# A third seven-product quad in the even gate/up blocks, and the down projection of a pair cut in two

## The chip, the core and the metric

One core of a Trainium2 chip runs the whole program. The metric is the device time of one execution in microseconds (us); several executions are timed and their median is given. Five engines matter. TensorE (PE) multiplies. VectorE (DVE) adds, subtracts and reads results out of PSUM. ScalarE (ACT) copies and applies functions. GpSimd (POOL) issues a few transfers. SyncE (SP) issues the weight loads. Each engine works through its own queue in a fixed order, and waits where an operand isn't ready.

## The reference, cut to what matters

Two decoder layers run over 256 tokens of width 2048 in float32. Each has a token mixer (sparse attention beside latent attention, not touched here), a layer norm, and a SwiGLU feed-forward part of width 5632 with a second layer norm:

```
def _swiglu(x, w_gate, w_up, w_down):
    h = jax.nn.silu(jnp.einsum('bsd,df->bsf', x, w_gate)) * jnp.einsum('bsd,df->bsf', x, w_up)
    return jnp.einsum('bsf,fd->bsd', h, w_down)
...
x = _layer_norm(ALPHA * x + mix, ln1_g[i], ln1_b[i])
ffn = _swiglu(x, w_gate[i], w_up[i], w_down[i])
x = _layer_norm(ALPHA * x + ffn, ln2_g[i], ln2_b[i])
```

## The kernel before

**Weights and units.** A float32 product is made of three matmuls of rounded parts: each operand is split in a high part and a rest, and high by high, high by rest and rest by high are summed. Weights come in units of 512 KB, two 128-row tiles of 512 columns. `load_raw` (L301) loads a unit from SP's queue into one of six `raw` buffers. `parts` (L308 and L309) makes `wh` on ACT and `wl` on DVE, into one of seven pairs of buffers (`UNITS` 5 and `MORE` 2). A unit against both token tiles is 12 matmuls of 512 columns, against one operand it is 6.

**Gate and up.** The 5632 hidden columns are done in eleven blocks `fc` of 512. Block 0 is done by `proj`. From block 1 on, `gate_up` takes the 2048 rows of weights in four quads. A quad is a 2 by 2 by 2 product: two token tiles, two row units `u` and `u + 4`, and the two columns gate and up. `plain_quad` does it with its eight products, as four weight units of 12 matmuls. `wino_quad` does it with seven products of 6 matmuls, `p1`, `p2`, `p5`, `p6`, `p7`, `p4`, `p3` in this order. For these, DVE forms four sums of raw weight units in place (`add`, L871), each weight operand is then split (seven pairs `wh`, `wl` where the plain quad has four), and the token operands `s1` to `s4` are sums made once for the layer by `sum_operands`. The order in a block is plain 0, wino 2, plain 1, wino 3.

**Ends of a block.** The products gather in eight PSUM banks, `c11` to `c22` and `p1` to `p7`. In the last quad of a block, eight DVE operations (L886 to L911, "finals" below) combine them: `g0` (L886) frees the bank `c11`, `g1` (L905) frees `c21`, and so on. The plain quad of the next block writes `c11` and `c21` first. `hidden` then applies silu (ACT), multiplies (DVE), transposes (PE) and splits the result to `hT`.

**Down.** After plain 0, `between` is called. In blocks 2, 4, 6 and 8 it runs `down` of the two finished blocks over all four output columns: 16 weight units of 12 matmuls. In the odd blocks nothing runs there. After block 10, `down` of blocks 8 and 9 runs over all columns, and `last_pass` does block 10.

**Sums.** `norm_T` leaves the transposed normalised `x` of chunks 1 and 3 in `kept`, two buffers of the `raw` tag, and until `sum_operands` has run, raw loads leave these two alone (`phase["held"]`). `sum_operands` runs between the gate and the up half of block 0.

The core of the quad loop is:

```
for i, (u, w) in enumerate(zip(plain, wino)):
    plain_quad(u, i == len(plain) - 1)
    if i == 0:
        between()
    r = wino_quad(w, i == len(wino) - 1)
```

Of the kernel before, what the change touches and what calls it, by code (L numbers as in the profile page):

```python
# [31 lines left out]
P = 128  # L32
D = 2048
# [24 lines left out]
RAWMORE = 2  # L58
HALF = NKT // KU // 2
T2 = 11  # L60
LASTU = 2


QI0, TA, QI1, TB, KA0, QA0, VA0, KA1, QA1, VA1 = range(10)
# [14 lines left out]
def hybrid_trunk(ctx: ExitStack, tc: tile.TileContext, x, xt_in, pos, w_in, g_cq, g_ckv, w_uq,  # L79
# [8 lines left out]
    def nm(s):  # L88
        uid[0] += 1
        return f"{s}{uid[0]}"  # L90
# [23 lines left out]
    def t2(shape, s, dt=F32):  # L114
        return sb.tile(shape, dt, name=nm(s), tag="t2", bufs=T2)
# [157 lines left out]
    def spawn(gen):  # L273
        task = [0, gen]
        tasks.append(task)
        step(task)
        return task
# [5 lines left out]
    def finish(*ends):  # L283
        while any(e in tasks for e in ends):
            for task in list(tasks):
                if any(e in tasks for e in ends):
                    step(task)


    def some(key, have, more):  # L290

        if phase["name"] == "more" and not (key == "raw" and phase.get("held")):
            phase[key] = phase.get(key, 0) + 1
            if phase[key] * more % (have + more) < more:
                return phase["pool"], more
        return sb, have
# [19 lines left out]
    def proj(units, lhs, n, before=None, split_t=None):  # L316

        o = [acc() for _ in range(NT)]  # L320
        loaded = []
        last = len(units) - 1

        def go(t, u):
            (wh, wl), ks = loaded[u], units[u][1]
            for j, k in enumerate(ks):
                h, l = lhs(t, k)
                a, b = wh[:, j, :n], wl[:, j, :n]
                first, final = u == 0 and j == 0, u == last and j == len(ks) - 1
                mm(o[t][:, :n], h, a, start=first, stop=False)  # L330
                mm(o[t][:, :n], h, b, start=False, stop=False)  # L331
                mm(o[t][:, :n], l, a, start=False, stop=final)  # L332

        for u, (src, ks) in enumerate(units):
            if before is not None:
                before(u)
            loaded.append(load_unit(src, src.shape[-1]))
            for t in range(1 if split_t else NT):
                go(t, u)
            tick()  # L340
        if split_t:
            split_t()
            for u in range(len(units)):
                go(1, u)
                tick()
        return o
# [5 lines left out]
    def split(hi, lo, src):  # L352
        nc.scalar.activation(hi, src, AF.Copy)
        nc.vector.tensor_tensor(lo, src, f(hi), op=ALU.subtract)  # L354
# [22 lines left out]
            nc.vector.tensor_scalar(y[:, sl], y[:, sl], mu, rs, ALU.subtract, ALU.mult)  # L377
            yield c, sl

    def norm_T(gbT, y, hi, lo, keep=None):  # L380


        for _ in normalise(y, moments(y)):
            pass
        yield 5
        for c in range(D // C):
            tp = trp()
            transpose4([y[:, c * C + i * P:c * C + (i + 1) * P] for i in range(4)], tp)
            if keep is not None and c in keep:
                v = keep[c]  # L390
            else:
                v = t2([P, 4, P], "v")
            for i in range(4):
                k = 4 * c + i
                nc.scalar.activation(v[:, i, :], tp[:, i * P:(i + 1) * P], AF.Identity,
                                     bias=gbT[:, 1, k:k + 1], scale=gbT[:, 0, k:k + 1])
            nc.vector.tensor_copy(hi[:, 4 * c:4 * c + 4, :], v)
            nc.vector.tensor_tensor(lo[:, 4 * c:4 * c + 4, :], v, f(hi[:, 4 * c:4 * c + 4, :]), op=ALU.subtract)
            yield 1
# [79 lines left out]
    def layer(l, xh, xl, norms, last):  # L479
# [296 lines left out]
        def then(t):  # L776
            xh.append(t8([P, NKT, P], F32R, "xh"))
            xl.append(t8([P, NKT, P], F32R, "xl"))
            norms.append(spawn(norm_T(gbT, xt[t], xh[t], xl[t], kept[t] if ffn[0] else None)))

        ffn, kept = [True], []
        phase["held"] = True
        for t in range(NT):
            v = phase["pool"].tile([P, 2, 4, P], F32, name=nm("kept"), tag="raw", bufs=RAWMORE)
            kept.append({1: v[:, 0], 3: v[:, 1]})
        last_pass(lambda c, k: w_o[l, c, k // KU], [4, 6], olhs, then)


# [2 lines left out]
        def gu(i, fc, split_t=None):  # L791
            return proj([(w_gu[i][l, fc, u], range(u * KU, (u + 1) * KU)) for u in range(NKT // KU)], xk, C,
                        None, split_t)
# [2 lines left out]

        def sum_operands():

            a = [[kept[t][c] for c in (1, 3)] for t in range(NT)]
            for name, x, y in (("s1", a[1][0], a[1][1]), ("s2", a[0][0], "s1"), ("s3", a[1][0], a[0][0]),  # L800
                               ("s4", a[0][1], "s2")):
                y = sums[y][2] if isinstance(y, str) else y
                v = t2([P, 4, P], "sv")
                nc.vector.tensor_tensor(v, x, y, op=ALU.subtract)
                hi, lo = (phase["pool"].tile([P, 4, P], F32R, name=nm(name), tag=name + p, bufs=1) for p in "hl")
                split(hi, lo, v)
                sums[name] = hi, lo, v
            phase["held"] = False

        def slhs(name):  # L810
            return lambda k: tuple(m[:, k % 4, :] for m in sums[name][:2])

        def hidden(gs, us, hT, tr):

# [16 lines left out]
        BANKS = {"c11": 4, "c21": 5, "c12": 6, "c22": 7, "p1": 0, "p5": 1, "p6": 2, "p7": 3}  # L831
        INTO = {"p2": "c11", "p4": "c21", "p3": "c12"}

        def gate_up(fc, plain, wino, between):


            o, begun = {}, set()
# [19 lines left out]
            def plain_quad(u, lastz):  # L857
                for i, col in enumerate(("c11 c21", "c12 c22")):
                    for v in (u, u + HALF):
                        w = load_unit(w_gu[i][l, fc, v], KU * C)  # L860
                        for t, name in enumerate(col.split()):
                            passes(name, token(t), unit(v), w, lastz and name == "c22" and v != u)
                        tick()
# [49 lines left out]
                if final:  # L913
                    return [g0, g1], [e, v]

            for i, (u, w) in enumerate(zip(plain, wino)):
                plain_quad(u, i == len(plain) - 1)
                if i == 0:
                    between()
                r = wino_quad(w, i == len(wino) - 1)  # L920
            return r

        def down(fcs, hTs, then):
            def lhs(t, k):
                h, j = hTs[k // 4], k % 4
                return h[:, 0, j, t * P:(t + 1) * P], h[:, 1, j, t * P:(t + 1) * P]

            units = C // P // KU * len(fcs)
            u0 = C // P // KU * fcs[0]
            if fcs[-1] == NFC - 1:  # L930
                units -= LASTU
            for c in range(D // C):
                o = proj([(w_down[l, c, u0 + u], range(u * KU, (u + 1) * KU)) for u in range(units)], lhs, C)
                for t in range(NT):
                    sl = xt[t][:, c * C:(c + 1) * C]
                    if fcs[0] == 0:
                        nc.vector.scalar_tensor_tensor(sl, sl, ALPHA, o[t], op0=ALU.mult, op1=ALU.add)
                    else:
                        d = t2([P, C], "d")
                        nc.scalar.activation(d, o[t], AF.Copy)  # L940
                        nc.gpsimd.dma_start(sl, d, accum_op=ALU.add)  # L941
            if fcs[-1] == NFC - 1:
                finish(*[h[2] for h in held])
                last_pass(lambda c, k: w_down[l, c, u0 + k // KU], [(units + i) * KU for i in range(LASTU)], lhs, then)

        def behind_ffn(t):
            if last:
# [10 lines left out]
        def free_banks(t):  # L958
            return bank(2 + t, "tr")

        def group():
            finish(*[h[2] for h in held])
            if len(held) == 2 and held[-1][0] < NFC - 2:
                down([h[0] for h in held], [h[1] for h in held], behind_ffn)
                held.clear()

        g = gu(0, 0, lambda: finish(*norms))
        sum_operands()
        affine(ln1_g[l], ln1_b[l], 0)
        u = gu(1, 0)  # L970
        affine(ln1_g[l], ln1_b[l], 1)
        spawn_hidden(0, g, u, free_banks)
        for fc in range(1, NFC):
            g, u = gate_up(fc, (0, 1), (2, 3), group)
            if fc == 1:
                affine(ln1_g[l], ln1_b[l], 2)
                affine(ln1_g[l], ln1_b[l], 3)
            spawn_hidden(fc, g, u, free_banks if fc < NFC - 1 else lambda t: trp())
        xh, xl, norms, ms = [], [], [], []
        ffn[0] = False  # L980
        if last:
            gb = [load_gb(ln2_g[l], ln2_b[l], slice(c * C, (c + 1) * C)) for c in range(D // C)]
        else:
            gbT = load_gbT(ln2_T[l])
        finish(*[h[2] for h in held[:2]])
        down([h[0] for h in held], [h[1] for h in held], behind_ffn)
        if last:
            for t in range(NT):
                norm_out(t, gb, ms[t])
# [57 lines left out]
```

## Time and profile before

| what | value |
|---|---|
| time, median of 3 runs | 2238.47 us (2237.68 to 2239.29) |
| profiled execution | 2240.56 us |
| its span, first to last instruction | 2238.5 us |
| PE busy | 2194.0 us, 98% |
| DVE busy | 1702.2 us, 76% |
| ACT busy | 1193.1 us, 53% |
| granted clock of PE, mean | 0.996 |

Matmuls overlap in the trace: one of 512 columns is recorded with about 0.39 us while the next starts 0.23 us after it. So the busy share of PE hides short gaps, and the starts in the timeline have to be read. In the timeline a row is: start in us, duration in us, engine, line, operation, output and inputs, count, and in brackets the idle time of the engine before it with what ended it. Several instructions of one kind in a row are merged.

### The profile page before, as it was taken

Reading aid. Unit: us, or ns where it says so; the run is one execution under the profiler, and the core shown is the slowest. Engines: PE = TensorE matmul, PEld = TensorE weight load, DVE = VectorE, ACT = ScalarE, POOL = GpSimd, SP = SyncE. Lnnn points to the kernel's source line nnn. Section 1 sums busy time; section 2 is a strip of 40 time slices with the busy share of each in tenths; the row PEclk is TensorE's granted clock in tenths of the full one; section 3 lists DMA queues with packets and bytes.
Section 4 is the critical chain, followed back from the end, with each engine's and each line's share of the span. In section 5 each row is a group of like instructions: output and inputs, shape, how many; then the busy total and the mean of one; then the engine's idle time right before and its main releaser. Section 6 shows DMA issues by size and latency. Waiting matters only on the chain. (4 is left out here: it accounts for less than half of the span.)

```text
span 2238.5 us, 27874 instructions
## 1 busy us (share of the span) xinstructions
PE 2194.0 (98%) x10128; PEld 1809.4 (81%) x10128; DVE 1702.2 (76%) x2215; ACT 1193.1 (53%) x1537; POOL 110.2 (5%) x198
## 2 busy tenths in 40 slices
PE   8999999999999999999999999999999999999997
PEld 7878788788888887887777887887888888888885
DVE  6675556987968788699667756569879697887985
ACT  5555443654555555555545554445546555555563
POOL 0100000100000000100101000001000100000002
PEclk9999999999999999999999999999999999999998
DMA  8544445656576766756655455556655757576574
GB/s 300 162 154 149 143 166 181 242 170 207 180 234 206 245 189 225 201 204 201 204 173 166 141 166 165 174 174 226 206 186 201 223 201 244 178 250 210 193 258 115
DMA packets 126057, 437.04 MB, mean 195 GB/s; under 512 B 14320, under 2 KB 14368, under 8 KB 125664
## 3 DMA queue, kind: packets, MB, share of 16 engines
q1 hardware_dynamic: 113760, 409.26, 54.0%
q0 software_dynamic: 12160, 26.01, 5.9%
q8 instruction: 79, 1.29, 0.2%
q14 instruction: 58, 0.48, 0.1%
HBM read 416.33 MB, written 2.10 MB: 187 GB/s over the span
## 5 line engine op out<-in xcount | busy, mean ns | idle before, releaser
L309 DVE TENSOR_TENSOR wl<-raw,wh 128x1024 fp32r<-128x1024 f32 (+1 forms) x892 | 1068.9, 1218 | 448.8 <-ACT wh L308 441.9
L308 ACT ACTIVATE wh<-raw 128x1024 fp32r<-128x1024 f32 (+1 forms) x892 | 926.9, 1055 | 873.9 <-PE acc L332 392.1
L846 PE MATMUL gu_c<-wh,xh 128*128 128x512 f32 x800 | 314.1, 393 | 6.7 <-DVE g L905 6.5
L848 PE MATMUL gu_c<-wl,xh 128*128 128x512 f32 x800 | 311.3, 389 | 0.0
L849 PE MATMUL gu_c<-wh,xl 128*128 128x512 f32 x800 | 311.3, 390 | 0.0
L330 PE MATMUL acc<-wh,xh 128*128 128x512 f32 (+1 forms) x768 | 303.0, 395 | 6.3 <-ACT wh L308 6.3
L331 PE MATMUL acc<-wl,xh 128*128 128x512 f32 (+1 forms) x768 | 299.1, 389 | 3.6 <-DVE wl L309 3.6
L332 PE MATMUL acc<-wh,xl 128*128 128x512 f32 (+1 forms) x768 | 297.9, 388 | 0.0
L330 PE MATMUL acc<-wh,hT 128*128 128x512 f32 x640 | 249.0, 389 | 0.9 <-DVE v L906 0.9
L331 PE MATMUL acc<-wl,hT 128*128 128x512 f32 x640 | 249.1, 389 | 0.5 <-DVE wl L309 0.5
L332 PE MATMUL acc<-wh,hT 128*128 128x512 f32 x640 | 248.8, 389 | 0.0
L871 DVE TENSOR_TENSOR raw<-raw,raw 128x1024 f32<-128x1024 f32 x160 | 195.5, 1223 | 8.4 <-DMA raw<-in_w_up_dram 5.0
L846 PEld LDWEIGHTS gu_c<-wh,xh 128*128 128x128 f32 x800 | 150.2, 188 | 41.0 <-DVE g L905 10.2
L849 PEld LDWEIGHTS gu_c<-wh,xl 128*128 128x128 f32 x800 | 150.2, 188 | 31.5
L330 PEld LDWEIGHTS acc<-wh,xh 128*128 128x128 f32 x768 | 144.7, 189 | 37.9 <-ACT wh L308 7.1
L848 PEld LDWEIGHTS gu_c<-wl,xh 128*128 128x128 f32 x800 | 150.2, 188 | 30.5 <-DVE wl L309 0.3
L331 PEld LDWEIGHTS acc<-wl,xh 128*128 128x128 f32 x768 | 145.3, 189 | 32.0 <-DVE wl L309 6.1
L332 PEld LDWEIGHTS acc<-wh,xl 128*128 128x128 f32 x768 | 145.0, 189 | 27.9
L330 PEld LDWEIGHTS acc<-wh,hT 128*128 128x128 f32 x640 | 120.1, 188 | 26.2 <-DVE v L906 1.3
L331 PEld LDWEIGHTS acc<-wl,hT 128*128 128x128 f32 x640 | 120.1, 188 | 25.7 <-DVE wl L309 0.9
L332 PEld LDWEIGHTS acc<-wh,hT 128*128 128x128 f32 x640 | 120.1, 188 | 24.9
L941 POOL DMA_DIRECT2D x<-d x64 | 55.0, 875 | 1135.4 <-ACT d L940 1108.5
(235 smaller groups left out, 2611.3 us busy)
## 6 DMA issues: line engine op xcount, KB each, us to landing
raw<-in_w_gate_dram SPq DMA_DIRECT2D x176, 512.0 KB, 4.7
raw<-in_w_up_dram SPq DMA_DIRECT2D x176, 512.0 KB, 4.7
raw<-in_w_down_dram SPq DMA_DIRECT2D x176, 512.0 KB, 5.1
raw<-in_w_in_dram SPq DMA_DIRECT2D x144, 512.0 KB, 3.4
raw<-in_w_o_dram SPq DMA_DIRECT2D x64, 512.0 KB, 3.3
x<-d POOLq DMA_DIRECT2D x64, 256.0 KB, 6.4
raw<-in_w_in_dram SPq DMA_DIRECT2D x16, 400.0 KB, 3.0
raw<-in_w_uq_dram SPq DMA_DIRECT2D x12, 512.0 KB, 3.3
```

Source lines behind the costliest of these rows:

```text
L308: nc.scalar.activation(wh[:, :n], raw[:, :n], AF.Copy)
L309: nc.vector.tensor_tensor(wl[:, :n], raw[:, :n], f(wh[:, :n]), op=ALU.subtract)
L330: mm(o[t][:, :n], h, a, start=first, stop=False)
L331: mm(o[t][:, :n], h, b, start=False, stop=False)
L332: mm(o[t][:, :n], l, a, start=False, stop=final)
L846: mm(o[name], h, a, start=name not in begun, stop=False)
L848: mm(o[name], h, b, start=False, stop=False)
L849: mm(o[name], l, a, start=False, stop=end)
L871: nc.vector.tensor_tensor(d, x, y, op=ADD)
L941: nc.gpsimd.dma_start(sl, d, accum_op=ALU.add)
```

## The change

Even blocks (2, 4, 6, 8 and 10) do quads 1, 2 and 3 as seven products, and quad 0 plain. Odd blocks keep two and two. `down` of a pair runs in two halves: columns 0 and 1 behind plain 0 of the even block, columns 2 and 3 behind plain 0 of the following odd block; columns 2 and 3 of the pair (8, 9) run after block 10. Each half is 8 weight units. Since quad 1 needs its sums too, `sum_operands` now covers all of row tiles 2 to 7 and 10 to 15, rebuilds its inputs as `xh + xl`, and moves behind the up half of block 0. `kept` and `held` go. `last_pass` takes all of block 10's rows as before.

```diff
-            a = [[kept[t][c] for c in (1, 3)] for t in range(NT)]
-            for name, x, y in (("s1", a[1][0], a[1][1]), ("s2", a[0][0], "s1"), ("s3", a[1][0], a[0][0]),
-                               ("s4", a[0][1], "s2")):
...
+            few = t8([P, 4, 2, 2, P], F32R, "few")
+            many = phase["pool"].tile([P, 4, 2, 4, P], F32R, name=nm("many"), tag="many", bufs=1)
+            for k0, n, where in ((4, 4, many), (2, 2, few)):
+                a = {}
+                for t in range(NT):
+                    for i in range(2):
+                        ks = slice(k0 + i * NKT // 2, k0 + i * NKT // 2 + n)
+                        v = a[t, i] = t2([P, n, P], "av")
+                        nc.vector.tensor_tensor(v, f(xh[t][:, ks, :]), f(xl[t][:, ks, :]), op=ALU.add)
+                prev = {}
+                for i, (x, y) in enumerate((((1, 0), (1, 1)), ((0, 0), "s1"), ((1, 0), (0, 0)), ((0, 1), "s2"))):
+                    v = prev[f"s{i + 1}"] = t2([P, n, P], "sv")
+                    nc.vector.tensor_tensor(v, a[x], prev[y] if isinstance(y, str) else a[y], op=ALU.subtract)
+                    hi, lo = where[:, i, 0], where[:, i, 1]
+                    split(hi, lo, v)
...
-            for i, (u, w) in enumerate(zip(plain, wino)):
-                plain_quad(u, i == len(plain) - 1)
+            lastp = max(i for i, q in enumerate(order) if q[0] == "plain")
+            for i, (kind, u) in enumerate(order):
+                if kind == "plain":
+                    plain_quad(u, i == lastp)
+                else:
+                    r = wino_quad(u, i == len(order) - 1)
                 if i == 0:
                     between()
-                r = wino_quad(w, i == len(wino) - 1)
...
-        def group():
-            finish(*[h[2] for h in held])
-            if len(held) == 2 and held[-1][0] < NFC - 2:
-                down([h[0] for h in held], [h[1] for h in held], behind_ffn)
-                held.clear()
+        def behind_quad(fc):
+
+            def go():
+                if fc < 2:
+                    return finish(*[h[2] for h in held])
+                down(held[:2], (0, 1) if fc % 2 == 0 else (2, 3))
+                if fc % 2:
+                    del held[:2]
+                finish(*[h[2] for h in held])
+            return go
+
+        ORDER = [[("plain", 0), ("wino", 1), ("wino", 2), ("wino", 3)],
+                 [("plain", 0), ("wino", 2), ("plain", 1), ("wino", 3)]]
...
-        sum_operands()
         affine(ln1_g[l], ln1_b[l], 0)
         u = gu(1, 0)
+        sum_operands()
...
-            g, u = gate_up(fc, (0, 1), (2, 3), group)
+            g, u = gate_up(fc, ORDER[fc % 2], behind_quad(fc))
...
-        finish(*[h[2] for h in held[:2]])
-        down([h[0] for h in held], [h[1] for h in held], behind_ffn)
+        down(held[:2], (2, 3))
+        finish(held[2][2])
+        u0 = C // P // KU * (NFC - 1)
+        last_pass(lambda c, k: w_down[l, c, u0 + k // KU], [0, KU], down_lhs([held[2][1]]), behind_ffn)
```

## Rows read from the trace of the kernel before

**Rows 1.** The page, its first part: busy time, share, instructions by engine.

```profile
PE 2194.0 (98%) x10128; PEld 1809.4 (81%) x10128; DVE 1702.2 (76%) x2215; ACT 1193.1 (53%) x1537; POOL 110.2 (5%) x198
```

**Rows 2.** Groups by line and form: busy us, mean ns, idle before and releaser.

```profile
L309 DVE TENSOR_TENSOR wl<-raw,wh 128x1024 fp32r<-128x1024 f32 x876 | 1053.0, 1222 | 429.8 <-ACT wh L308 423.2 <-issue 0.2
...
L871 DVE TENSOR_TENSOR raw<-raw,raw 128x1024 f32<-128x1024 f32 x160 | 195.5, 1223 | 8.4 <-DMA raw<-in_w_up_dram 5.0
...
L905 DVE TENSOR_TENSOR g<-gu_c,v 128x512 f32<-128x512 f32 x20 | 13.7, 685 | 0.0
```

**Rows 3.** Waits of PE: us in total, times, longest.

```profile
PE gu_c L846 <- DVE g L905: 6.5, 6, 1.7
...
PE acc L331 <- DVE wl L309: 4.1, 4, 1.2
```

**Rows 4.** Timeline of PE, last quad of block 3, layer 0.

```profile
607.41 0.39 PE L846 MATMUL gu_p<-wh,xh 128*128 128x512 f32 x1
...
611.49 0.39 PE L846 MATMUL gu_p<-wh,s 128*128 128x512 f32 x1
...
616.93 0.39 PE L846 MATMUL gu_c<-wh,xh 128*128 128x512 f32 x1
...
619.81 0.50 PE L846 MATMUL gu_c<-wh,xh 128*128 128x512 f32 x1 [0.45 <-DVE g L905]
```

**Rows 5.** Timeline of DVE, for the same quad.

```profile
599.07 2.50 DVE L309 TENSOR_TENSOR wl<-raw,wh 128x1024 fp32r<-128x1024 f32 x2 [1.25 <-ACT wh L308]
...
607.59 4.63 DVE L309 TENSOR_TENSOR wl<-raw,wh 128x1024 fp32r<-128x1024 f32 x4
612.13 0.68 DVE L886 TENSOR_TENSOR g<-e,gu_c 128x512 f32<-128x512 f32 x1
612.73 2.36 DVE L309 TENSOR_TENSOR wl<-raw,wh 128x1024 fp32r<-128x1024 f32 x2
...
619.07 0.69 DVE L905 TENSOR_TENSOR g<-gu_c,v 128x512 f32<-128x512 f32 x1
```

**Rows 6.** Timeline of DVE: block 1's first unit; block 2's quad behind the down projection.

```profile
438.17 4.63 DVE L309 TENSOR_TENSOR wl<-raw,wh 128x1024 fp32r<-128x1024 f32 x4
...
530.08 1.23 DVE L309 TENSOR_TENSOR wl<-raw,wh 128x1024 fp32r<-128x1024 f32 x1 [1.49 <-ACT wh L308]
...
546.45 1.23 DVE L309 TENSOR_TENSOR wl<-raw,wh 128x1024 fp32r<-128x1024 f32 x1 [0.30 <-ACT wh L308]
```

**Rows 7.** Timeline of PE at the first matmuls of the same three units.

```profile
448.08 0.39 PE L846 MATMUL gu_c<-wh,xh 128*128 128x512 f32 x1
...
545.11 0.39 PE L846 MATMUL gu_c<-wh,xh 128*128 128x512 f32 x1
...
553.45 0.39 PE L846 MATMUL gu_c<-wh,s 128*128 128x512 f32 x1
```

**Rows 8.** Windows: us, then busy us of PE, PEld, DVE, ACT, POOL, clock, DMA.

```profile
426.00:444.00 18.00, 18.00 (x82) 14.88 (x80) 15.34 (x17) 11.71 (x12) 1.07 (x2) 1.00 0.97 357
...
545.10:554.60 9.50, 9.50 (x43) 7.63 (x42) 8.22 (x8) 7.21 (x7) 0.00 (x0) 1.00 0.83 253
...
587.00:596.50 9.50, 9.50 (x43) 7.88 (x42) 9.47 (x9) 7.93 (x8) 0.00 (x0) 1.00 0.59 175
...
607.40:616.90 9.50, 9.50 (x43) 7.88 (x42) 9.50 (x11) 7.81 (x10) 0.00 (x0) 1.00 0.68 225
```

**Rows 9.** Windows around two gaps of PE, with the granted clock.

```profile
110.00:122.00 12.00, 8.87 (x42) 6.08 (x40) 9.43 (x21) 4.69 (x9) 0.00 (x0) 0.86 0.42 136
...
870.00:876.00 6.00, 4.30 (x19) 3.25 (x19) 6.00 (x9) 4.50 (x5) 0.00 (x0) 1.00 0.87 327
```

**Rows 10.** DMA issues (us to landing), and DVE's waits for a transfer.

```profile
raw<-in_w_up_dram SPq DMA_DIRECT2D x176, 512.0 KB, 4.7
...
DVE raw L871 <- DMA raw<-in_w_up_dram: 5.0, 7, 0.9
```

More of the change, by code (lines that the diff above doesn't have):

```diff
@@ L60 @@
 T2 = 11
-LASTU = 2
 QI0, TA, QI1, TB, KA0, QA0, VA0, KA1, QA1, VA1 = range(10)
@@ L290, in some @@
     def some(key, have, more):
-        if phase["name"] == "more" and not (key == "raw" and phase.get("held")):
+        if phase["name"] == "more":
             phase[key] = phase.get(key, 0) + 1
@@ L378, in normalise, with norm_T @@
             yield c, sl
-    def norm_T(gbT, y, hi, lo, keep=None):
+    def norm_T(gbT, y, hi, lo):
         for _ in normalise(y, moments(y)):
@@ L388, in norm_T @@
             transpose4([y[:, c * C + i * P:c * C + (i + 1) * P] for i in range(4)], tp)
[L389 to L392, printed above, removed]
+            v = t2([P, 4, P], "v")
             for i in range(4):
@@ L778, in then @@
             xl.append(t8([P, NKT, P], F32R, "xl"))
[L779 to L785, printed above, removed]
+            norms.append(spawn(norm_T(gbT, xt[t], xh[t], xl[t])))
         last_pass(lambda c, k: w_o[l, c, k // KU], [4, 6], olhs, then)
@@ L797, in sum_operands @@
         def sum_operands():
-            a = [[kept[t][c] for c in (1, 3)] for t in range(NT)]
-            for name, x, y in (("s1", a[1][0], a[1][1]), ("s2", a[0][0], "s1"), ("s3", a[1][0], a[0][0]),
-                               ("s4", a[0][1], "s2")):
[L802 to L808, printed above, removed]
+            few = t8([P, 4, 2, 2, P], F32R, "few")
[13 more added lines that the diff above has]
+                    split(hi, lo, v)
+                    for k in range(n):
+                        sums[f"s{i + 1}", k0 + k] = hi[:, k, :], lo[:, k, :]
         def slhs(name):
-            return lambda k: tuple(m[:, k % 4, :] for m in sums[name][:2])
+            return lambda k: sums[name, k]
         def hidden(gs, us, hT, tr):
@@ L832, in layer, with gate_up @@
         INTO = {"p2": "c11", "p4": "c21", "p3": "c12"}
-        def gate_up(fc, plain, wino, between):
+        def gate_up(fc, order, between):
             o, begun = {}, set()
@@ L914, in wino_quad, with down_lhs @@
                     return [g0, g1], [e, v]
-            for i, (u, w) in enumerate(zip(plain, wino)):
-                plain_quad(u, i == len(plain) - 1)
+            lastp = max(i for i, q in enumerate(order) if q[0] == "plain")
[4 more added lines that the diff above has]
+                    r = wino_quad(u, i == len(order) - 1)
                 if i == 0:
                     between()
-                r = wino_quad(w, i == len(wino) - 1)
             return r
-        def down(fcs, hTs, then):
+        def down_lhs(hTs):
             def lhs(t, k):
@@ L926, in lhs, with down @@
                 return h[:, 0, j, t * P:(t + 1) * P], h[:, 1, j, t * P:(t + 1) * P]
[L928 to L933, printed above, removed]
+            return lhs
+        def down(pair, cols):
+            fcs, hTs = [h[0] for h in pair], [h[1] for h in pair]
+            finish(*[h[2] for h in pair])
+            per = C // P // KU
+            for c in cols:
+                o = proj([(w_down[l, c, per * fcs[0] + u], range(u * KU, (u + 1) * KU))
+                          for u in range(per * len(fcs))], down_lhs(hTs), C)
                 for t in range(NT):
@@ L941, in down @@
                         nc.gpsimd.dma_start(sl, d, accum_op=ALU.add)
-            if fcs[-1] == NFC - 1:
-                finish(*[h[2] for h in held])
-                last_pass(lambda c, k: w_down[l, c, u0 + k // KU], [(units + i) * KU for i in range(LASTU)], lhs, then)
         def behind_ffn(t):
@@ L959, in free_banks @@
             return bank(2 + t, "tr")
-        def group():
-            finish(*[h[2] for h in held])
-            if len(held) == 2 and held[-1][0] < NFC - 2:
-                down([h[0] for h in held], [h[1] for h in held], behind_ffn)
-                held.clear()
+        def behind_quad(fc):
[9 more added lines that the diff above has]
+                 [("plain", 0), ("wino", 2), ("plain", 1), ("wino", 3)]]
         g = gu(0, 0, lambda: finish(*norms))
-        sum_operands()
         affine(ln1_g[l], ln1_b[l], 0)
         u = gu(1, 0)
+        sum_operands()
         affine(ln1_g[l], ln1_b[l], 1)
@@ L979, in layer @@
         xh, xl, norms, ms = [], [], [], []
-        ffn[0] = False
         if last:
```

## The prediction, made before the changed kernel ran

> **What bounds the kernel now.** I read the page first: TensorE is busy for 98% of the span, VectorE for 76% [rows 1]. That says that fewer matmuls should mean less time. But these are averages over stages, so I next read the timelines of both engines over one quad, and then the windows. The reader is to see three things there.
>
> First, what a quad costs on each side. In the last quad of block 3, `p1` starts at 607.41, `p6` three products later at 611.49, and the next block at 616.93 [rows 4]. A product of 6 matmuls is 4.08 / 3 = 1.36 us, a seven-product quad 9.52 us, a plain one (eight) 10.88 us. VectorE runs through the same quad from 599.07 to 612.13, that is 13.06 us [rows 5]: seven `wl` and four sums. So inside such a quad VectorE is slower than TensorE by 13.06 - 9.52 = 3.5 us. The windows agree: in the two such quads of block 3 VectorE is busy for 9.47 and 9.50 of 9.5 us [rows 8]. The 76% of the page hide a stage in which VectorE has no slack at all.
>
> Second, how this is paid for. VectorE is ahead. I call lead the time from the end of a `wl` to the first matmul of its product. In block 3's last quad it is 607.41 - 600.29 = 7.1 us at `p1` (the first `wl` of the pair at 599.07 ends 1.22 us later) and 611.49 - 608.81 = 2.7 us at `p6` [rows 4, 5]: a fall of 4.4, because all four sums come before `p6`. After `p6` each product gives back 1.36 less the `wl`'s spacing of some 1.14 (13.06 less four sums of 1.22, by seven [rows 2, 5], is 1.17; the four in a row give 4.54 / 4 [rows 5]). A plain or down unit lasts 2.72 us against one `wl`, and gives back 1.6.
>
> Third, how far ahead it can be. Behind the down projection the lead is 545.11 - 531.31 = 13.8 us at `p1` of block 2, and at that quad's `p3` 553.45 - 547.68 = 5.8 us [rows 6, 7]. It fell by 8.0, more than the deficit of 3.5, and in that quad VectorE had time to spare: 8.22 of 9.5 us busy [rows 8]. It stood waiting for ACT's `wh`, which waits for a free pair of buffers. There are seven pairs, and seven products are consumed in 9.5 us where seven down units last 19. So however long the cover before it, the lead that a quad hands on is about 5.8 us.
>
> TensorE's own waits in the gate/up blocks are few: 6.5 us in all at `c21` for `g1` (L905), the longest 1.7 [rows 3].
>
> **The change, part by part.**
>
> *Fewer matmuls.* Ten blocks (five a layer) lose one product of 6 matmuls: 10 x 1.36 = 13.6 us of TensorE, 60 matmuls. This holds in full, as TensorE runs its starts back to back.
>
> *Down in halves.* The same 176 units and the same transfers to `x`, in other places. Odd blocks get 8 units of cover behind plain 0, as only even ones had. The 6.5 us at `c21` [rows 3] follow quads of odd blocks that had no down before them; I take all of them as recovered. Eight units give back 8 x 1.6 = 12.6 us of lead, near the ceiling of 13.8, so halving costs the even block nothing at its first seven-product quad. The queue of POOL gets the same transfers, spread out: nothing.
>
> *Three quads in a row.* Per even block VectorE gets three more `wl` and four sums, ACT three more `wh` (ACT is busy 7.8 of 9.5 us in such a quad [rows 8], so it holds). I follow the lead. The first quad hands on 5.8 (ceiling). At `p1` of the second: 5.8 + 0.2 = 6.0. One quad later, at `p1` of the third: 6.0 - 3.5 = 2.5. At its `p6`: 2.5 - 4.4 = -1.9. In this last quad `g0`, 0.6 us by the spacing 612.13 to 612.73 [rows 5], comes due before `p6` as well: -2.5. The matmul that needs `wl` is the second of a product, 0.2 later, so TensorE stands for 2.3 us. Bounds: 1.1 (`g0` not in front, and half a `wl` less), and 3.2 with one late transfer, as VectorE's longest wait for one is 0.9 [rows 10].
>
> [...]
>
> *The finals behind it.* The lead is then nil, and the eight finals must still pass VectorE, eight by 0.6 = 4.8 us, while the next block's plain quad waits for its `wl` and for `c21`. In block 3, with a lead of 2.7 at `p6`, `g1` started at 619.07 and TensorE waited 0.45 us until 619.81 [rows 4, 5]. With no lead the same order costs up to 0.45 + 2.7 = 3.2. Lower bound 1.7, the longest such wait seen [rows 3]; upper 4.8, all eight in front. I take 2.9, near the worked 3.2: the wait comes late in the unit and some of it is covered. After block 10 down units follow instead; I count it alike.
>
> So an even block stalls 2.3 + 2.9 = 5.2 us (2.8 to 8.0) and saves 1.36.
>
> *The sums, moved and widened.* VectorE does 24 operations per layer instead of 8. Even if each took a final's 0.6 us, that is 9.6 us more, now queued ahead of the `wl` of block 1. That lead is 448.08 - 439.39 = 8.7 us, and VectorE idles another 2.7 us in the stretch before [rows 6 to 8]. I cost it at nothing; without that cover it is up to 3 us a layer. The two raw buffers freed early may remove some of TensorE's 4.1 us of waits for `wl` [rows 3]; nothing taken.
>
> **The sum.** 10 x (5.2 - 1.36) = 38.4, less 6.5 recovered: +31.9 us. By the bounds: 10 x 1.44 - 6.5 = +8, and 10 x 6.64 - 6.5 = +60. The profiled execution took 2240.56 for a span of 2238.5, 0.1% above the median of 2238.47; from the median: 2270.4, between 2246 and 2298.
>
> **The rivals.**
>
> *Covered after all: faster.* If the 13.8 us of lead behind the down projection carried through, three quads would use 3 x 3.5 = 10.5 of it and nothing would stall. Then 13.6 + 6.5 are gained: 2218. For it: the leads behind down are large. Against: the fall from 13.8 to 5.8 in one quad while VectorE idled. It decides at the third quad's `p1`: above 5.0 us of lead there no stall follows. 0.10.
>
> *A draw.* If idle slots of the first quad (9.5 - 8.2 = 1.3 us) take sums of the second, and finals fall between later `wl`, a block stalls some 2 us: 10 x 0.64 - 6.5, about 2238. Against: a sum overwrites a raw unit that `p1` must have read first. 0.07.
>
> *Raw units late.* Three quads in a row want 4 units per 13 us, and each waits for a buffer that the quad before frees at `p4`; landing takes 4.7 us [rows 10], while VectorE has about four operations (4.7 us) until it needs it. One us late per quad adds 20 to 30 us: about 2295. 0.06.
>
> *The clock falls.* [...] 0.05.
>
> **How the numbers follow.** My forecast has 0.72 and spans 2246 to 2298; the likeliest is 2270. The clock's case lies within the range and half of the late units' too; the draw is at the edge. The range 2240 to 2297 leaves out the faster case and the tails. A measurement here tells about 0.2%, some 4.5 us, from no change. Faster 0.10, same 0.07, slower 0.83 (forecast, late units and clock).
>
> **What the profile after would show.** 60 matmuls fewer; VectorE with 70 more operations in the quads and 32 in the sums. In odd blocks, no wait at `c21` behind their last quad. In even blocks, TensorE standing for `wl` (L309) at `p6` of the third quad by 2 us, then for `g1` or a `wl` at the start of the next block by 3. If the first is missing, my ceiling on the lead is wrong; if the second is, the finals hide better than I think. If TensorE waits in block 1, the sums weren't hidden.

## The result, and the profile after

The changed kernel takes 2264.16 us (median of 4 runs, 2262.82 to 2266.95) against 2238.88 us (4 runs, 2237.68 to 2240.53). The ratio is 1.0114, with an interval of 1.0096 to 1.0132: slower by 25.5 us (21.5 to 29.6). Forecast were +31.9 us and 2270.4, within 2240 to 2297.

The page of the profiled execution, its span and its first part, stands against [rows 1]:

```profile
span 2262.9 us, 27869 instructions
...
PE 2202.4 (97%) x10068; PEld 1807.9 (80%) x10068; DVE 1796.7 (79%) x2317; ACT 1226.9 (54%) x1575; POOL 110.3 (5%) x198
```

TensorE has 60 matmuls fewer (10068 for 10128), VectorE 102 operations more, as counted beforehand. Yet TensorE's busy time rose by 8.4 us. Sixty matmuls fewer can't do that; either the starts lie further apart or the clock was lower. Its waits, in the view that groups them (us in total, times, longest), answer to [rows 3]:

```profile
PE gu_p L845 <- ACT wh L307: 12.0, 10, 1.4
...
PE gu_p L847 <- DVE wl L308: 5.5, 3, 1.8
...
PE gu_c L845 <- ACT wh L307: 3.5, 7, 0.8
...
PE gu_c L847 <- DVE wl L308: 1.2, 3, 0.6
```

The reader is to see two things. The waits at `c21` for `g1`, 6.5 us before, are gone altogether. And there are 22.2 us of new waits for weight operands inside the gate/up blocks, 2.2 in the mean for each of the ten even blocks: 17.5 at the banks of `p5` to `p7` (the rows of `gu_p`), 4.7 at those that follow (`gu_c`).

Where they lie is read from block 4 of the first layer. First VectorE's timeline, from the end of the first seven-product quad to the `p6` of the third:

```profile
656.95 3.51 DVE L308 TENSOR_TENSOR wl<-raw,wh 128x1024 fp32r<-128x1024 f32 x3 [1.93 <-ACT wh L307]
...
667.62 5.92 DVE L308 TENSOR_TENSOR wl<-raw,wh 128x1024 fp32r<-128x1024 f32 x5
673.46 2.48 DVE L870 TENSOR_TENSOR raw<-raw,raw 128x1024 f32<-128x1024 f32 x2
675.89 2.49 DVE L308 TENSOR_TENSOR wl<-raw,wh 128x1024 fp32r<-128x1024 f32 x2
678.29 0.68 DVE L885 TENSOR_TENSOR g<-e,gu_c 128x512 f32<-128x512 f32 x1
678.89 1.22 DVE L870 TENSOR_TENSOR raw<-raw,raw 128x1024 f32<-128x1024 f32 x1
680.02 1.22 DVE L308 TENSOR_TENSOR wl<-raw,wh 128x1024 fp32r<-128x1024 f32 x1
681.16 1.22 DVE L870 TENSOR_TENSOR raw<-raw,raw 128x1024 f32<-128x1024 f32 x1
682.29 3.49 DVE L308 TENSOR_TENSOR wl<-raw,wh 128x1024 fp32r<-128x1024 f32 x3
```

The `wh` of `p6`, from ACT's:

```profile
680.14 1.06 ACT L307 ACTIVATE wh<-raw 128x1024 fp32r<-128x1024 f32 x1 [1.59 <-DVE raw L870]
```

Then TensorE's, at the first products of the second and the third quad, at the product in front of the stall, and at the stall:

```profile
664.69 0.39 PE L845 MATMUL gu_p<-wh,xh 128*128 128x512 f32 x1
...
674.23 0.39 PE L845 MATMUL gu_p<-wh,xh 128*128 128x512 f32 x1
...
678.42 0.39 PE L845 MATMUL gu_p<-wh,many 128*128 128x512 f32 x1
...
679.58 0.39 PE L848 MATMUL gu_p<-wh,many 128*128 128x512 f32 x1
681.25 0.50 PE L845 MATMUL gu_p<-wh,many 128*128 128x512 f32 x1 [1.28 <-ACT wh L307]
683.57 0.80 PE L847 MATMUL gu_p<-wl,many 128*128 128x512 f32 x1 [1.82 <-DVE wl L308]
```

At 656.95 VectorE has just stood 1.93 us for ACT's `wh`, which waits for a pair of buffers: the ceiling. The second of the three `wl` there is the second quad's `p1`. It ends at 659.3, and TensorE uses it at 664.69: a lead of 5.4 (worked out: 6.0). From then on VectorE does not stop once until behind the stall. The fourth of the five at 667.62 is the third quad's `p1`. It ends at 672.4, for 674.23: 1.8 are left (worked out: 2.5). Then come two sums, two `wl`, `g0`, and the sum at 678.89 that `p6` needs. Its `wh` on ACT starts behind that sum, at 680.14, and is ready at 681.2. TensorE, free at 679.8, stands. `g0` in front of that sum costs its 0.6 us, as foreseen.

Two things here were not foreseen. The product at 678.42 starts before the sum that `p6` needs, so it isn't `p6`: in the changed program `p7` runs in front of it, and takes up 1.36 us of the lateness. And TensorE stands a second time, at 683.57, for the `wl` of `p6`. The `wl` at 680.02 starts before `p6` has its `wh` (680.14), so it is another unit's; it and the fourth sum (681.16) stand in VectorE's queue ahead of the `wl` of `p6`, the first of three at 682.29, which ends at 683.5. In this block the stall at `p6` is so 1.28 + 1.82 = 3.1 us. The second wait comes in three of the ten blocks. In block 10 of the first layer it is counted at a down unit that the program places inside the quad, outside the 22.2 us:

```profile
1079.10 0.79 PE L329 MATMUL acc<-wh,hT 128*128 128x512 f32 x1 [2.06 <-ACT wh L307]
```

The third thing is in the windows (us, busy us of PE, PEld, DVE, ACT, POOL, clock, DMA): the second quad, the stretch from the third quad's start to the next block's, and the same stretch of block 4 in the second layer.

```profile
664.60:674.20 9.60, 9.60 (x44) 7.87 (x43) 9.49 (x9) 4.97 (x5) 0.00 (x0) 1.00 0.56 181
674.20:690.00 15.80, 12.70 (x43) 9.53 (x42) 15.40 (x16) 10.09 (x11) 0.00 (x0) 0.78 0.58 198
1800.30:1814.00 13.70, 11.99 (x45) 9.18 (x44) 13.28 (x14) 9.46 (x10) 0.00 (x0) 0.88 0.48 165
```

VectorE is busy 15.4 of 15.8 us, and behind the stall TensorE's granted clock is 0.78 of full, 0.88 in the other layer: it fell for a part of the stretch. From 684 to 688 it was 0.50, and the matmuls of 512 columns started 0.43 us apart, where they start 0.23 apart at 1.00. Over the two stretches that is 15.8 x 0.22 = 3.5 and 13.7 x 0.12 = 1.6 us of TensorE's time. The ends of the first three even blocks of the first layer show how it goes on:

```profile
543.00:560.00 17.00, 13.93 (x54) 9.33 (x53) 16.93 (x20) 11.67 (x13) 0.00 (x0) 1.00 0.59 187
674.00:690.00 16.00, 12.90 (x44) 9.72 (x43) 15.61 (x16) 10.09 (x11) 0.00 (x0) 0.79 0.59 200
806.00:822.00 16.00, 12.59 (x47) 9.22 (x46) 15.61 (x16) 10.09 (x11) 0.00 (x0) 0.89 0.59 198
```

Only the first of the ten keeps 1.00; in the nine others it is 0.79 or from 0.89 to 0.90. Over the whole run the mean clock of 0.988 loses 27 us, where 0.996 before lost 9: 18 more.

Whether the low clock costs time can be read from block 2, which kept its clock, beside block 4, where it took 3.5 us. The first matmul of `p1` in a block's last quad marks the same point in every block. It starts in blocks 2, 3 and 5 at

```profile
543.17 0.39 PE L845 MATMUL gu_p<-wh,xh 128*128 128x512 f32 x1
...
612.07 0.39 PE L845 MATMUL gu_p<-wh,xh 128*128 128x512 f32 x1
...
744.01 0.39 PE L845 MATMUL gu_p<-wh,xh 128*128 128x512 f32 x1
```

and in block 4 at 674.23 (above). From block 2 to 3 that is 68.9 us, from block 4 to 5 69.8. So of the 3.5 us some 0.9 show in the time. Block 2 waits instead, in smaller pieces, and behind `p6` too; the longest of these are

```profile
552.44 0.50 PE L845 MATMUL gu_c<-wh,xh 128*128 128x512 f32 x1 [0.83 <-ACT wh L307]
...
558.22 0.50 PE L847 MATMUL gu_c<-wl,xh 128*128 128x512 f32 x1 [0.64 <-DVE wl L308]
```

### The profile page after: what moved, and what is told of

Same layout as the page of the kernel before. It is cut to its first block, busy times and chain, and to the rows that moved or that the text cites. A ratio compares the mean times of both kernels' runs of the same rounds, so it can differ in the third digit from the quotient of the medians.

```text
span 2262.9 us, 27869 instructions
## 1 busy us (share of the span) xinstructions
PE 2202.4 (97%) x10068; PEld 1807.9 (80%) x10068; DVE 1796.7 (79%) x2317; ACT 1226.9 (54%) x1575; POOL 110.3 (5%) x198
## 4 chain that ended last, share of the span: by engine, by line
PE 86%; DVE 8%; issue 2%; ACT 2%; DMA 1%; POOL 0%; ACTq 0%; DVEq 0%; SPq 0%
PE acc L329 16%; PE acc L330 16%; PE acc L331 16%; PE gu_c L845 7%; PE gu_c L847 7%; PE gu_c L848 7%; DVE wl L308 3%; PE gu_p L847 3%; DVE raw L870 3%; PE gu_p L848 3%; PE gu_p L845 2%; PE tr L349 2%; ACT wh L307 2%; DMA raw<-in_w_up_dram 1%; PE att L649 1%
## 5 line engine op out<-in xcount | busy, mean ns | idle before, releaser
L307 ACT ACTIVATE wh<-raw 128x1024 fp32r<-128x1024 f32 (+1 forms) x922 | 959.3, 1056 | 863.6 <-PE acc L331 357.5
L308 DVE TENSOR_TENSOR wl<-raw,wh 128x1024 fp32r<-128x1024 f32 (+1 forms) x922 | 1103.4, 1217 | 367.5 <-ACT wh L307 360.0
L845 PE MATMUL gu_c<-wh,xh 128*128 128x512 f32 x680 | 268.7, 397 | 0.8 <-ACT wh L307 0.8
L847 PE MATMUL gu_c<-wl,xh 128*128 128x512 f32 x680 | 266.3, 392 | 1.2 <-DVE wl L308 1.2
L848 PE MATMUL gu_c<-wh,xl 128*128 128x512 f32 x680 | 265.8, 391 | 0.0
L870 DVE TENSOR_TENSOR raw<-raw,raw 128x1024 f32<-128x1024 f32 x200 | 244.5, 1223 | 14.0 <-DMA raw<-in_w_up_dram 9.8
L845 PEld LDWEIGHTS gu_c<-wh,xh 128*128 128x128 f32 x680 | 129.6, 191 | 28.7 <-ACT wh L307 1.8
L847 PEld LDWEIGHTS gu_c<-wl,xh 128*128 128x128 f32 x680 | 128.5, 189 | 28.3 <-DVE wl L308 2.3
L848 PEld LDWEIGHTS gu_c<-wh,xl 128*128 128x128 f32 x680 | 128.3, 189 | 27.1
```

Source lines behind the costliest of these rows:

```text
L307: nc.scalar.activation(wh[:, :n], raw[:, :n], AF.Copy)
L308: nc.vector.tensor_tensor(wl[:, :n], raw[:, :n], f(wh[:, :n]), op=ALU.subtract)
L845: mm(o[name], h, a, start=name not in begun, stop=False)
L847: mm(o[name], h, b, start=False, stop=False)
L848: mm(o[name], l, a, start=False, stop=end)
L870: nc.vector.tensor_tensor(d, x, y, op=ADD)
```

## The experiments

The theory: VectorE can't keep up over three seven-product quads in a row, since the seven pairs of buffers cap the lead with which the second begins. Rivals: the cut of the down projection or the new sums carry the loss; raw units land too late; the fallen clock is the loss. Ratios are to the kernel before on the same chip.

**The third quad taken back.**

```diff
-        ORDER = [[("plain", 0), ("wino", 1), ("wino", 2), ("wino", 3)],
+        ORDER = [[("plain", 0), ("wino", 2), ("plain", 1), ("wino", 3)],
```

> The changed kernel with the third seven-product quad taken back: even blocks do two plain and two seven-product quads like odd ones; the halves of the down projection and the widened sums stay. Theory (VectorE cannot keep up in a third quad in a row; halving the cover costs nothing and removes the waits at the start of even blocks): 2238.9 less 6.5 us, 2232 (2229 to 2236), no stall inside the gate/up blocks, no fall of TensorE's clock there. Rival (the halving or the widened sums carry the loss): 2245 or more.

2231.87 us, ratio 0.9961 (0.9948 to 0.9974). No gate/up wait for a weight operand is left, and none at `c21`. So the halves gain some 9 us, and the third quad costs 1.0114 - 0.9961, 1.5% or some 34 us. This tells the parts of the change apart: one is good, the other bad.

**The third quad alone**, the down projection whole behind the even blocks.

```diff
-                down(held[:2], (0, 1) if fc % 2 == 0 else (2, 3))
-                if fc % 2:
-                    del held[:2]
                 finish(*[h[2] for h in held])
+                if fc % 2 == 0 and fc < NFC - 1:
+                    down(held[:2], range(4))
+                    del held[:2]
...
-        down(held[:2], (2, 3))
+        down(held[:2], range(4))
```

> The changed kernel with the down projection whole again behind plain 0 of the even blocks and nothing behind the odd ones. Theory: the third quad stalls as in the changed kernel, and the odd block that follows starts with no lead and no cover, so it waits as well: 2270 to 2285. Rival (halving the cover is what starves the third quad): at or below 2250.

2290.23 us, ratio 1.0226 (1.0208 to 1.0245), a little above the range. TensorE's first row of waits is now

```profile
PE gu_p L845 <- ACT wh L307: 24.8, 36, 1.4
```

36 waits where the changed kernel has 10: the odd blocks wait too. The halving is what keeps the third quad from costing still more.

**Work in the stalls**: zero times something, added to the banks of `p6` and `p7`.

```diff
+        FILL = {"p6": 6, "p7": 6}
...
+                    if final and fc % 2 == 0 and i in FILL:
+                        for _ in range(FILL[i]):
+                            mm(o[name], zeror, xh[0][:, 0:4, :], start=False, stop=False)
```

> The changed kernel with twelve matmuls by a zero operand (six ahead of p6, six ahead of p7) in the last quad of each even block, 120 in all, 27 us of TensorE's time; the sums that they add are zero. They put work into the stalls. [...] Rival (VectorE alone sets the time there, and a slower TensorE only waits less): 2264 within 4 us, or up to 27 us more if the stalls have no room.

2259.72 us, ratio 1.0081 (1.0068 to 1.0093): 120 matmuls more (27 us of TensorE) and still 4 us faster by the medians, 7 by the ratios. The added work, two of the waits that are left, and the long window of the first layer's blocks (same columns as above):

```profile
L882 PE MATMUL gu_p<-xh,zeror 128*128 128x512 f32 x120 | 31.4, 395 | 0.0
```

```profile
PE gu_c L850 <- DVE g L912: 3.6, 2, 2.2
...
PE gu_p L850 <- ACT wh L311: 2.0, 5, 0.6
```

```profile
500.00:1090.00 590.00, 584.32 (x2577) 476.46 (x2576) 511.95 (x493) 329.83 (x357) 24.06 (x28) 1.00 0.65 203
```

The waits for weight operands shrank to 3.2 us in all, the clock was 1.00 over the window (0.98 in the changed kernel's same window) and 0.995 over the whole run (0.988), and 27 us of work found room in the gaps. But giving TensorE its clock back returned far less than the 18 us that it had lost. Most of the low clock only replaced waiting, as blocks 2 and 4 showed above: VectorE set the time. The 4 to 7 us are net of what the added matmuls cost where they found no gap, which was not separated. Had the fall of the clock been a loss of its own, up to 18 us would have come back, down to 2246 us; the rival, that VectorE alone sets the time, had 2264 within 4. The truth lies between, nearer the rival.

**VectorE relieved in the last quad**: the four sums left out there, transfers and matmuls kept.

```diff
                 def add(d, x, y):
+                    if final and fc % 2 == 0:
+                        return
                     nc.vector.tensor_tensor(d, x, y, op=ADD)
```

> The changed kernel without the four sums of raw weights in the last quad of each even block (left out of the computation, so the products of that quad take the raw units as they are): VectorE has some 4.8 us less there, transfers and matmuls stay. Theory (VectorE's work is the limit): the stalls and the fall of the clock vanish, 2238.9 less 13.6 less 6.5 plus a few us of waits, 2219 to 2225. Rival (raw units come late, three quads in a row want too many): the stalls stay, above 2245.

2216.29 us, ratio 0.9889 (0.9874 to 0.9903), slightly below the range. The stalls are gone, with three quads in a row and every transfer in place. So raw units were not what was late. Against the kernel with two quads (0.9961) that is 16 us less, near the 13.6 of the saved product: this is what the third quad gives when VectorE has room. The edit also takes away the step from a sum to its `wh`, so it doesn't tell VectorE's amount of work from the order in which its queue does it. A changed kernel with the sum and the `wl` of `p6` placed earlier in that queue was not run.

**One pair of buffers fewer, one more.** For the eighth pair, room is needed: the token sums `few` of quad 1 and one `a8` buffer are dropped. The kernel with these dropped and seven pairs is its control.

```diff
-UNITS, MORE = 5, 2
+UNITS, MORE = 4, 2
```

> The changed kernel with six pairs of wh and wl instead of seven. If the lead that a quad hands on is set by the pairs, it falls by one product, 1.36 us, to some 4.4, and each of the ten third quads stalls that much longer: 2264 plus 10 to 18 us, 2274 to 2282. Rival (VectorE's rate alone matters, the pairs don't): within 4 us of 2264.

```diff
-UNITS, MORE = 5, 2
+UNITS, MORE = 6, 2
...
-        return sb.tile(shape, dt, name=nm(s), tag="a8", bufs=10)
+        return sb.tile(shape, dt, name=nm(s), tag="a8", bufs=9)
...
-            few = t8([P, 4, 2, 2, P], F32R, "few")
-            for k0, n, where in ((4, 4, many), (2, 2, few)):
+            for k0, n, where in ((4, 4, many),):
...
-            return lambda k: sums[name, k]
+            return lambda k: sums[name, max(k, 4 + k % 2)]
```

> The changed kernel with eight pairs of wh and wl. The room comes from leaving out the token sums of quad 1 (it takes those of quad 2 instead, which spares VectorE 12 small operations a layer that were hidden). If the pairs set the lead, it rises by 1.36 us and each third quad stalls that much less, with fewer falls of the clock: 2264 less 12 to 18, 2246 to 2252. Rival (pairs don't matter): within 4 us of 2264.

> The changed kernel without the token sums of quad 1 (left out: quad 1 takes those of quad 2), with seven pairs: the control for the kernel with eight. If the eighth pair made the 25 us: 2264 within 3. Rival (the sums left out made a part): 2250 to 2260.

Six pairs: 2278.60 us, ratio 1.0164 (1.0149 to 1.0179). Eight: 2238.87, ratio 0.9993 (0.9984 to 1.0003). The control: 2268.95, ratio 1.0125 (1.0112 to 1.0139), a little above the expected range. The waits for weight operands with six pairs, then with eight:

```profile
PE gu_p L845 <- ACT wh L307: 19.4, 20, 1.8
PE gu_p L847 <- DVE wl L308: 10.5, 9, 1.9
...
PE gu_c L845 <- ACT wh L307: 2.6, 5, 0.6
...
PE gu_c L847 <- DVE wl L308: 1.5, 4, 0.6
```

```profile
PE gu_p L844 <- ACT wh L307: 5.2, 9, 1.3
...
PE gu_c L846 <- DVE wl L308: 2.8, 9, 0.6
PE gu_p L846 <- DVE wl L308: 1.6, 4, 0.6
PE gu_c L844 <- ACT wh L307: 1.5, 4, 0.5
```

34.0 us with six pairs, 22.2 with seven, 11.1 with eight: some 1.1 to 1.2 us a block for each pair, near the 1.36 of one product. The pairs set the lead: at the second quad's `p1` of block 4, read as above, it is 4.2 us with six (`wl` done at 662.1, used at 666.3), 5.4 with seven, 6.5 with eight (656.3 and 662.8). The time fell by more at eight, 1.0125 - 0.9993 or 30 us; some 9 of these are also seen with two quads (below, 0.9984 to 0.9945), where no gate/up wait for a weight operand is left to be shortened, so most likely elsewhere than at the stalls.

**Sums on GpSimd**, first `r12`, then `r12` and `r21`, in the even blocks.

```diff
-                    nc.vector.tensor_tensor(d, x, y, op=ADD)
+                    eng = nc.gpsimd if fc % 2 == 0 and d is r12 else nc.vector
+                    eng.tensor_tensor(d, x, y, op=ADD)
```

> The changed kernel with one of the four sums of a seven-product quad (r12) on GpSimd in the even blocks, three quads each. If GpSimd can add beside VectorE, a quad is 1.2 us shorter on VectorE, the lead at the third quad's p6 rises by some 3 us, and the stalls mostly vanish: 2222 to 2235. Rival (the two engines hold each other up, or GpSimd's sum is late): 2255 or more.

> As the kernel before this one, with two of the four sums (r12 and r21) on GpSimd. If GpSimd adds freely: 2217 to 2228, below the kernel with one. Rival (GpSimd's time per sum, some 3 us by its 1.6 us for half the size at the end of the kernel, lies on the path from r12 to p7 and r21 to p4): slower than with one.

2285.33 us, ratio 1.0200 (1.0183 to 1.0217), and 2317.62, ratio 1.0342 (1.0327 to 1.0358). My hope was wrong by 50 us or more. In the first of them, by line and form, and in TensorE's waits:

```profile
L308 DVE TENSOR_TENSOR wl<-raw,wh 128x1024 fp32r<-128x1024 f32 x906 | 1132.3, 1272 | 364.4 <-ACT wh L307 358.4 <-issue 0.2
...
L871 POOL TENSOR_TENSOR raw<-raw,raw 128x1024 f32<-128x1024 f32 x30 | 73.4, 2446 | 805.9 <-ACT wh L307 345.2 <-DMA raw<-in_w_gate_dram 288.9 <-DVE raw L871 138.4
```

```profile
PE gu_p L847 <- DVE wl L308: 25.7, 24, 1.8
```

A sum takes 2.45 us on GpSimd, and VectorE's `wl` got slower: 1272 ns in the mean where it was 1222, that is 906 x 50 ns = 45 us in all, more than the 30 x 1.22 = 37 us of sums that it was spared. How much of the loss is this and how much the later `r12` was not separated.

**Two quads, the halves, and what the room buys.** With two quads a block `few` isn't needed, so the eighth pair fits with the whole computation kept. The second kernel is the same with seven pairs; both give up one `a8` buffer.

```diff
-        ORDER = [[("plain", 0), ("wino", 1), ("wino", 2), ("wino", 3)],
+        ORDER = [[("plain", 0), ("wino", 2), ("plain", 1), ("wino", 3)],
...
-UNITS, MORE = 5, 2
+UNITS, MORE = 6, 2
...
-        return sb.tile(shape, dt, name=nm(s), tag="a8", bufs=10)
+        return sb.tile(shape, dt, name=nm(s), tag="a8", bufs=9)
...
-            few = t8([P, 4, 2, 2, P], F32R, "few")
-            for k0, n, where in ((4, 4, many), (2, 2, few)):
+            for k0, n, where in ((4, 4, many),):
```

> Two seven-product quads in every block and the halves of the down projection, with eight pairs of wh and wl: since quad 1 is plain, its token sums are not needed, and their room gives the eighth pair. The whole computation is kept. Theory: no stall is left in the gate/up blocks for the pair to remove; a little less waiting elsewhere: 2226 to 2232, the fastest. Rival (a deeper lead helps everywhere, as eight pairs took 25 us off the three-quad kernel): 2220 or less.

> As the kernel before this one, with seven pairs: the halves alone, without the unneeded token sums of quad 1. If those sums were hidden: 2232 within 2. Rival (they cost): 2 to 6 us less.

With eight pairs 2227.72 us, ratio 0.9945 (0.9932 to 0.9957): faster than both kernels, and the lowest median with the whole computation, though its interval overlaps that of the halves with seven pairs and `few` (0.9948 to 0.9974). With eight pairs too the third quad doesn't pay: 0.9993 with it, 0.9945 without. With seven and `few` dropped 2237.08, ratio 0.9984 (0.9975 to 0.9992), some 5 us slower than with `few`. It makes less and takes longer, which neither expectation had. The timeline of TensorE tells where: the first matmul of block 1 starts, with `few` and ten `a8` buffers, and then without and nine, at

```profile
448.44 0.39 PE L845 MATMUL gu_c<-wh,xh 128*128 128x512 f32 x1
```

```profile
451.27 0.39 PE L844 MATMUL gu_c<-wh,xh 128*128 128x512 f32 x1
```

Some 2.8 us of it are lost before the first `gate_up`. The `a8` buffer that was given up serves the mixer too; that this is the cause is argued, not shown. A like loss stands between the control of the pairs and the changed kernel: 5 us by the medians, 2 to 3 by the ratios.

**The sums alone**: two quads, the down projection whole, only the widened and moved sums and the two `raw` buffers no longer held. Against the changed kernel, the edit is those of the first two experiments together. Against the kernel before, the move is left, and the widening that the change shows:

```diff
-        sum_operands()
         affine(ln1_g[l], ln1_b[l], 0)
         u = gu(1, 0)
+        sum_operands()
...
```

> The kernel before with the widened and moved sums alone: two seven-product quads, the whole down projection behind the even blocks, no buffers held. If the halving removed the waits at c21: these waits stay (some 6 us) and the time is that of before, within 3 us. Rival (the sums and the freed raw buffers made the gain of the halves): 2230 to 2235.

2240.32 us, ratio 0.9995 (0.9986 to 1.0004): no change. The wait at `c21` is there, as before:

```profile
PE gu_c L845 <- DVE g L904: 5.3, 8, 1.5
```

So it was the halving that removed it, and the sums are hidden.

## Why the prediction was right, step by step

**The bound and its place.** Right. Within three quads VectorE is the limit: with the sums of one quad away the loss turns into a gain of 1.1%, while buffers, transfers and matmuls are as they were, and with one pair of buffers more or less the waits shrink or grow.

**The ceiling on the lead.** Right, and the step on which the sign hung. The lead behind the first quad was 5.4 where 6.0 was worked out, and 1.8 where 2.5. Waits follow the number of pairs: 34.0, 22.2, 11.1 us for six, seven, eight. The rival "covered after all" fails here: the lead at the third quad's `p1` was 1.8, and 5.0 were needed. One row behind this step was misread: the matmul at 545.11 [rows 7] writes `gu_c`, so it isn't the first of `p1`. In block 4 of the changed kernel, behind the down units, the rows of `p1` give the same 655.17 - 641.42 = 13.8 us:

```profile
640.20 1.22 DVE L308 TENSOR_TENSOR wl<-raw,wh 128x1024 fp32r<-128x1024 f32 x1 [1.50 <-ACT wh L307]
```

```profile
655.17 0.39 PE L845 MATMUL gu_p<-wh,xh 128*128 128x512 f32 x1
```

**The stall at `p6`, 2.3 us a block.** Measured some 1.75 in the mean (the 17.5 us of `gu_p`): 3.1 in block 4, 1.3 where only the first of the two waits comes. The place is right. The rows name ACT's `wh` for most of it, not `wl`: `p6` needs the sum first, then `wh`, then `wl`, so its lateness shows at the earlier of the two, and at both where another unit's `wl` and a sum stand in between. The working had `p6` in the source's order; the program had put `p7` in front of it, which hid a product's length of the lateness.

**The saved product, 13.6 us.** Some 16 us by the kernel that leaves VectorE room, within its interval.

**Halving.** Forecast 6.5 us recovered, measured some 9 (6 to 12). It costs nothing, as the lead is full again behind eight units (the 13.8 us above).

**The sums.** Nothing, as forecast.

**The wait at `c21` behind the third quad, 2.9 us a block.** This step failed. No matmul of the changed kernel waits for `g1`, and with the clock held up by filler only two do, 3.6 us. I had carried a wait over from a program order in which it stood, with less lead; but the finals are placed anew in the changed program, and around 686 in block 4 `e` (L893) even waits for TensorE by 0.32 us. What stood there in its place is, in block 2, more waiting for weight operands, 2.2 of its 2.9 us of waits. In the nine other even blocks most of it is the fall of the clock, which I had given a chance of 0.05. It took 18 us of TensorE's time, but it doesn't come on top of the waits: 0.9 of 3.5 us by blocks 2 to 5, and 4 to 7 of the 18 by the filler kernel, net. While VectorE is behind, a slower TensorE mostly waits less.

**The sum.** Third quads cost some 34 us by the ratios; with the 13.6 saved that is 4.8 us a block, where 5.2 stood in the sum. Of the 4.8, 2.4 are recorded waits (22.2 us and the 2.06 of block 10, by ten) and 1.8 (18 us by ten) time at the low clock. The rest is not accounted for; the overlap of the matmuls' records hides some 0.16 us (0.39 less 0.23) of every gap. That the total came out close is partly luck: one wrong term (2.9 at `c21`) stood where another loss was.

**Late raw units.** Not the cause: the transfers are unchanged in the kernel that is fastest. VectorE's waits for a transfer in front of its sums rose only from 5.0 [rows 10] to 9.8 us in all.

## What to carry to other kernels

Before trading TensorE work for VectorE work, compare the two engines over the one stage where the trade is made, not over the page. Where VectorE is slower there (13.1 us a quad for TensorE's 9.5 here), the lead with which the stage begins pays for it, and that lead is capped by the buffers between the engines, counted in time of the consumer: a long cover before the stage doesn't help beyond it (in block 4 the 13.8 us of lead behind the down units were 5.4 at the next seven-product quad). Cover spread evenly (the halved down projection) did help, by some 9 us, and an eighth pair of buffers took away most of what the third quad cost (1.0125 with seven, 0.9993 with eight). And the order of a queue matters where there is no lead: `p6` waited behind work of VectorE that was needed later, 1.82 us in block 4.

## What the runs showed of the hardware that was not expected

Two stalls in short succession, the first of 1.1 to 1.4 us and the second of 0.4 to 2.1, went with a fall of TensorE's clock in nine of ten even blocks, to 0.79 or from 0.89 to 0.90 over 16 to 17 us; in block 2 pieces of up to 0.8 us left it at 1.00. In the kernel before, the clock was 0.86 over the 12 us around a single gap of 3.13 us, and 1.00 over the 6 us around one of 1.70 [rows 9]:

```profile
117.10 0.47 PE L350 MATMUL tr<-ident,dup 128*128 128x128 f32 x1 [3.13 <-DVE ckvT L354]
...
875.30 0.50 PE L846 MATMUL gu_c<-wh,xh 128*128 128x512 f32 x1 [1.70 <-DVE g L905]
```

With 120 matmuls by a zero operand in the places of the stalls it was 1.00 in the mean over the first layer's blocks. Of 18 us of TensorE's time lost to the low clock, 4 to 7 us came back with them, net of what they cost. A float32 sum of 128 x 1024 took 2446 ns on GpSimd and 1223 on VectorE, and with thirty of them on GpSimd the mean `wl` rose from 1222 ns in the kernel before to 1272.
